# One down tile of each small expert slot in native fp32, an eighth load buffer, and a token table reduced earlier

## The chip, the cores and the metric

The kernel runs on one core of a Trainium2 chip. The metric is the device time of one execution in microseconds (us). The engines are PE (TensorE, matrix products, with its weight loads PEld), DVE (VectorE), ACT (ScalarE), POOL (GpSimd) and SP (SyncE, which only issues transfers here).

## The reference

One decoder block: 512 tokens and 16 meta tokens of width 1024 go through a hybrid mixer (FoX attention and RWKV-7 side by side), then through a mixture of 32 experts of which each token takes four, with LayerNorm after each. The change lies in the mixture:

```python
def moe_ffn(h, w_router, b_router, w_gu, b_gu, w_down, b_down):
    logits = (h @ w_router + b_router).astype(jnp.float32)
    top_vals, top_idx = lax.top_k(logits, TOP_K)
    gates = jax.nn.softmax(top_vals, axis=-1)
    ...
    def expert_block(args):
        xblk, e = args
        gu = xblk @ w_gu[e] + b_gu[e]
        gate, up = gu[:, :D_EXPERT], gu[:, D_EXPERT:]
        gate = jnp.minimum(gate, SWIGLU_LIMIT)
        up = jnp.clip(up, -SWIGLU_LIMIT, SWIGLU_LIMIT)
        act = (up + 1.0) * (gate * jax.nn.sigmoid(gate * SWIGLU_ALPHA))
        return act @ w_down[e] + b_down[e]
```

Everything is float32. Each expert has 1024 x 2048 gate and up weights (8 MB) and 1024 x 1024 down weights (4 MB), so 384 MB of weights pass through the core.

## The kernel before, in words

The mixer takes the first 480 us or so. After it the router ranks the experts, tokens are entered in a table by expert, and the 32 experts are worked through as 32 *slots*, sorted by their number of tokens. `KINDS = "BBS" + "SB" * 14 + "B"` (L43) names them: a big slot (B) holds up to 112 tokens, a small one (S, 15 of them: slots 2, 3, 5, 7, ... 29) up to 64. From slot 3 on a small and a big slot take turns; such a pair is the unit in which the trace repeats.

*Tiles.* A slot has eight gate/up tiles, called ko0 to ko7 (`gtile`, L1427), and four down tiles, c0 to c3 (`dtile`, L1437). Each is 128x2048 float32, 1 MB, and is loaded by SP into a `raw` buffer. Seven such buffers are used in turn: `RAW = 5` in one pool and `RAW2 = 2` in another.

*Split.* float32 products are made from two fp32r parts. `split_w` (L1013) writes the high part `wh` with a copy on ACT (recorded at L130) and the low part `wl = raw - wh` with a subtraction on DVE (L1019); there are five buffers for each. A `raw` buffer is free once the subtraction has read it. `spl` holds the last two split instructions.

*Matmuls.* All go through the helper `mm` (L100). In a big slot the activations also have a high and a low part, and a product takes three passes. In a small slot the high and low parts of 64 tokens stand side by side as 128 stationary columns, so that two passes (`wh`, `wl`) do; rows 0 to 63 of the result hold the product with the high part, rows 64 to 127 that with the low part, and `put` adds them.

*A slot's turn* (the loop from L1722): the gate/up matmuls (`gu_stage`); the splits of down tiles c0 and c1 of the slot before (`PD = 2`); the activation, `swiglu` for a big slot (ACT `sgm`, DVE `act` at L1482 and L1483), `halves` for a small one; the transposes of the next slot's tokens (`flip_pair` gives `xs` for a small slot, `flip` gives `xTh` and `xTl` for a big one); then the down matmuls of the slot before, with the splits of c2 and c3 (`down_stage`); the splits of the next slot's ko0 and ko1 (`PG = 2`); and `put`, which scales the result by the gates and adds it to the output by an indirect DMA on POOL (L1569). For a small slot `put` is two instructions on ACT (`yl`) and two on DVE (`yo`, L1566). Last comes the second half of the activation: `flip` of `act` (PE transposes, then `aTh` on ACT, `aTl` on DVE at L1387) for a big slot, `swiglu_pair` for a small one, which ends in `at` (128 x 8 x 64, float32) and `a2`, its high and low part.

*What sets the order.* A scheduler orders each engine's instructions within the data dependences; `order(i, j)` puts i behind j, and `held` puts the activation and `put` behind the last split (`hold`), so that the splits run ahead.

*The table.* Tokens are scattered in rounds into four tables, which POOL copies into `tab4`. In slot 0's turn `listed` (L1361) reduces them on DVE over the four tables: a minimum gives the token numbers, a maximum the gates:

```python
V.tensor_reduce(lst[:, 0], tab4[:, :, :, 0].rearrange("p k c -> p c k"), AX.X, OP.min)
V.tensor_reduce(lst[:, 1], tab4[:, :, :, 1].bitcast(F32).rearrange("p k c -> p c k"), AX.X, OP.max)
```

`take` (L1276) makes `xTh`, `xTl` of slots 0 and 1. `xz` (L1310) is a zeroed tile that ACT's queue writes to the padding rows of two DRAM tensors, 512 KB each. The one-hot tile `ohs` (`onehot`, L1372) serves the last slots.

Of the kernel before, what the change touches and what calls it, by code (L numbers as in the profile page):

```python
# [9 lines left out]
F32 = mybir.dt.float32  # L10
F32R = mybir.dt.float32r
# [12 lines left out]
D = 1024  # L24
# [41 lines left out]
FAFTER = (0, 1, 3)  # L66
FOXG = (2, 4, 8, 8)
RAW = 5
RAW2 = 2
MLO = 3  # L70
MLL = 2
MHI = 3
# [2 lines left out]
PRE = 8  # L75
PD = 2
PG = 2

C_MU, C_W0, C_A0, C_KK, C_KA, C_RK, C_BF, C_G0, C_B0, C_G1, C_B1, C_N = 0, 14, 18, 22, 26, 30, 34, 35, 43, 51, 59, 67

# [13 lines left out]
def hybrid_block(ctx, tc, x, meta, win, wf, wout, cvec, lw, g2, lnp, gnp, wr, br,  # L94
# [4 lines left out]
    def mm(o, l, r, start, stop):  # L99
        return T.matmul(o, l, r, start=start, stop=stop, skip_group_check=True)  # L100
# [1169 lines left out]
    xp = pool(ctx, "xT", 2, "right")  # L1270
    mhr = pool(ctx, "mhr", MHR, "right")

    def xt_tile():
        return [xp.tile([128, KO, 128], F32R, tag=n, name=n) for n in ("xTh", "xTl")]

    def take(ps):  # L1276
        xT = xt_tile()
        for f0 in (0, 4):
            pv = ps[f0 // 4].rearrange("p (a b) -> p a b", b=128)
            a = actv(xT[0][:, f0:f0 + 4], pv, AF.Copy)  # L1280
            v = V.tensor_tensor(xT[1][:, f0:f0 + 4], pv, f32(xT[0][:, f0:f0 + 4]), OP.subtract)
        return xT, a, v

    xT, xci, xvi = take(ps0)
    xT1 = take(ps1)[0]
    rp = bank()
    for j in range(4):
        mm(rp[:, 0:NE], oneb, selb[:, j, :], j == 0, j == 3)
# [69 lines left out]
        V.tensor_copy(eidt, ps[0:1, 2 * NE:3 * NE])  # L1358
        V.tensor_copy(capr, ps[:, NE:2 * NE])

    def listed():  # L1361
        lst = mp2.tile([NE, 2, C], F32, name="lst")
        V.tensor_reduce(lst[:, 0], tab4[:, :, :, 0].rearrange("p k c -> p c k"), AX.X, OP.min)
        V.tensor_reduce(lst[:, 1], tab4[:, :, :, 1].bitcast(F32).rearrange("p k c -> p c k"), AX.X, OP.max)
        ps = small_ps()
        for j in range(2):
            mm(ps[0:C, NE * j:NE * j + NE], lst[:, j], perm, True, True)
        V.tensor_copy(idxs[0:C], ps[0:C, 0:NE])
        V.tensor_copy(gates[0:C], ps[0:C, NE:2 * NE])
        V.tensor_copy(gates[H:2 * H, NE - NSM:], ps[0:H, 2 * NE - NSM:2 * NE])  # L1370
# [16 lines left out]
            tail[3] = V.tensor_tensor(lo[:, f0:f0 + 4], pv, f32(h), OP.subtract)  # L1387
        return hi, lo

    xgt = xp.tile([128, D], F32, name="xg", bufs=1)  # L1390
    G.memset(xgt, 0.0)

    def fetch(idx, n):
# [43 lines left out]
    def dtile(sl, c):  # L1437
        raw = raw_tile()
        nc.sync.dma_start(raw, w_down[expert(sl), c].rearrange("o p n -> p (o n)"))
        after = None  # L1440
        if sl == NE - 2 and c == 3:
            after = (None, tail[0])
        if sl == NE - 1 and c:
            after = (tail[2] if c > 1 else None, tail[3])
        dw[sl, c] = split_w(raw, after)

    def gu_stage(sl, xT):
        small = KINDS[sl] == "S"
# [25 lines left out]
    hold = [None, None]  # L1474

    def swiglu(ps):
        act = wk.tile([128, D], F32, tag="act", name="act")[0:C]
        for n in range(2):
            s = slice(512 * n, 512 * n + 512)
            sg = wk.tile([128, 512], F32, tag="sgm", name="sgm", bufs=2)[0:C]  # L1480
            held(actv(sg, ps[n], AF.Silu, scale=SALPHA), 0)
            held(V.tensor_scalar(act[:, s], ps[2 + n], 1.0 - LIM, 1.0 + LIM, op0=OP.max, op1=OP.min), 1)  # L1482
            tail[0] = V.scalar_tensor_tensor(act[:, s], sg, SALPHA * LIM * SIGLIM, act[:, s], op0=OP.min, op1=OP.mult)  # L1483
        return act
# [7 lines left out]
    def swiglu_pair(gt):  # L1492
        pt = []
        for j in range(2):
            ps = psT.tile([128, 512], F32, tag="tr", name="tr")
            for f in range(KO):
                mm(ps[:, H * f:H * f + H], gt[:, D * j + 128 * f:D * j + 128 * f + 128], fold, True, True)
            pt.append(ps)
        sg = wk.tile([128, 512], F32, tag="sgm", name="sgp", bufs=2)
        actv(sg, pt[0], AF.Silu, scale=SALPHA)  # L1500
        at = wk.tile([128, D], F32, tag="act", name="at")[:, 0:512]
        V.tensor_scalar(at, pt[1], 1.0 - LIM, 1.0 + LIM, op0=OP.max, op1=OP.min)
        V.scalar_tensor_tensor(at, sg, SALPHA * LIM * SIGLIM, at, op0=OP.min, op1=OP.mult)
        a2 = wk.tile([128, KO, 2, H], F32R, tag="aTh", name="a2")
        av = at.rearrange("p (k c) -> p k c", c=H)
        actv(a2[:, :, 0, :], av, AF.Copy)
        V.tensor_tensor(a2[:, :, 1, :], av, f32(a2[:, :, 0, :]), OP.subtract)
        return a2

    def down_stage(sl, aT):  # L1510
        small = KINDS[sl] == "S"
        pl, rows_ = PLACE[sl], 128 if small else C
        ps = [psD.tile([128, 512], F32, tag="dn", name="dn")[0:rows_] for _ in range(2)]
        for c in range(4):
            if (sl, c) not in dw:
                dtile(sl, c)
            w = dw.pop((sl, c))
            for k in range(2):
                for a, b in ((0, 0), (1, 0)) if small else PASS:
                    for n in range(2):  # L1520
                        st_ = aT[:, 2 * c + k].rearrange("p a c -> p (a c)") if small else aT[b][:, 2 * c + k, :]
                        i = mm(ps[n], st_, w[a][:, D * k + 512 * n:D * k + 512 * n + 512],
                               c == k == a == b == 0, c == 3 and k == 1 and a == 1)
                        if sl == NE - 2 and c == 3 and k == a == b == n == 0:
                            order(i, tail[1])
        return ps, gates[0:rows_, pl:pl + 1], idxs[0:H if small else C, pl:pl + 1]
# [195 lines left out]
    for sl in range(NE):  # L1722
        nxt = KINDS[sl + 1] if sl + 1 < NE else None
        if sl and nxt:
            n, pl = H if nxt == "S" else C, PLACE[sl + 1]
            xg = fetch(idxs[0:n, pl:pl + 1], n)
        if sl == NE - 2:
            oh = onehot(FIXED[2], G)
        small, final = KINDS[sl] == "S", sl == NE - 1
        gu = gu_stage(sl, xT)  # L1730
        if sl == 0:
            ranked()
            listed()
        if pend is not None:
            for c in range(PD):
                dtile(pend[0], c)
            hold[:] = spl
        act = (halves if small else swiglu)(gu)
        if sl == PRE:
            prepare()  # L1740
        if sl == 0:
            xT = xT1
        elif nxt:
            xT = flip_pair(xg) if nxt == "S" else flip(xg, [t[:, :, 0:C] for t in xt_tile()])
        if final:
            aT = flip(act, [t[:, :, 0:C] for t in xt_tile()])
        if pend is not None:
            dn = down_stage(*pend)
            if nxt:
                for k in range(PG):  # L1750
                    gtile(sl + 1, k)
                hold[:] = spl
            else:
                hold[:] = [None, None]
            put(*dn, KINDS[pend[0]] == "S")
        pend = (sl, aT if final else swiglu_pair(act) if small else flip(act))
        if sl == TBL:
            tables()
# [83 lines left out]
```

## Time and profile before

| | |
|---|---|
| median of three runs | 1661.18 us (1655.45 to 1666.61) |
| profiled execution | 1652.43 us, of which its span is 1650.7 us |
| mean granted TensorE clock | 0.961 |
| busy share of the span | PE 92%, DVE 82%, ACT 63%, POOL 20% |
| bytes moved | 470 MB in all, mean 285 GB/s |

The profiled execution lies 8.75 us under the median of the runs and just below the fastest of them. The table shows averages; the mixer and the slots have different limits, so that the slots have to be read by themselves.

### The profile page before, as it was taken

What the parts mean: (1) busy time and instruction counts of PE and PEld (TensorE: products, weight loads), DVE (VectorE), ACT (ScalarE), POOL (GpSimd) and SP (SyncE); (2) the same over time, 40 slices, a digit from 0 to 9 for tenths busy, and PEclk for the clock granted to TensorE, in tenths of its full rate; (3) what the DMA queues carried; (4) which work ended last, traced back from release to release, by engine and by line L of the source; (5) the groups of instructions that cost most, each with busy time, mean ns of one, the idle gap of its engine ahead of it and who ended that gap; (6) DMA issues with size and microseconds to landing.
All of it is one profiled execution on the core that took longest, in us unless ns stands there. A gap on an engine that the chain in (4) does not pass through costs nothing.

```text
span 1650.7 us, 22742 instructions
## 1 busy us (share of the span) xinstructions
PE 1525.8 (92%) x8375; PEld 1199.1 (73%) x8375; DVE 1352.7 (82%) x1470; ACT 1036.9 (63%) x1059; POOL 327.6 (20%) x236
## 2 busy tenths in 40 slices
PE   4999999999997999999999999999999999999992
PEld 3799997786785777677676776767767677676761
DVE  8377584477887989988989889898898988989884
ACT  4444232234335778787877777777777777777762
POOL 5011201024443415111111111111211112111002
PEclk9799995799998999999999999999999999999996
DMA  4222313002667999999999999999999999999963
GB/s 180 75 77 77 79 52 84 1 20 88 243 210 269 324 382 418 403 397 381 383 386 393 375 369 391 388 396 370 375 393 382 396 369 375 386 385 389 372 227 128
DMA packets 89236, 469.90 MB, mean 285 GB/s; under 512 B 21676, under 2 KB 22716, under 8 KB 39938
## 3 DMA queue, kind: packets, MB, share of 16 engines
q1 hardware_dynamic: 76608, 444.51, 69.3%
q0 software_dynamic: 7136, 19.42, 5.2%
q10 hardware_dynamic: 5378, 4.50, 1.0%
q8 instruction: 67, 1.10, 0.3%
q14 instruction: 47, 0.39, 0.1%
HBM read 446.78 MB, written 24.53 MB: 286 GB/s over the span
## 4 chain that ended last, share of the span: by engine, by line
PE 32%; DVE 19%; issue 10%; ACT 3%; DMA 3%; POOL 0%; DVEq 0%; POOLq 0%; ACTq 0%
PE gu L100 18%; DVE wl L1019 15%; PE dn L100 10%; PE tr L100 3%; ACT wh L130 2%; DMA raw<-in_w_gu_dram 2%; DVE yo L1566 1%; DVE act L1483 1%; DMA raw<-in_w_down_dram 1%; DVE xTl L1387 1%; DVE aTl L1387 1%; ACT sgm L130 0%; PE tr L1403 0%; PE pc L100 0%; ACT raw L130 0%
## 5 line engine op out<-in xcount | busy, mean ns | idle before, releaser
L1019 DVE TENSOR_TENSOR wl<-raw,wh 128x2048 fp32r<-128x2048 f32 x384 | 859.8, 2282 | 93.7 <-ACT wh L130 92.5
L130 ACT ACTIVATE wh<-raw 128x2048 fp32r<-128x2048 f32 x384 | 709.7, 1914 | 46.1 <-PE gu L100 13.5
L1569 POOL DMA_INDIRECT yd<-yo,idxs x31 | 81.8, 2640 | 573.0 <-DVE yo L1566 404.3
L100 PE MATMUL gu<-wl,xs 128*128 128x512 f32 x480 | 142.5, 418 | 33.8 <-DVE wl L1019 28.7
L100 PE MATMUL gu<-wl,xTh 128*112 128x512 f32 x544 | 149.6, 394 | 9.0 <-DVE wl L1019 9.0
L1395 POOL DMA_INDIRECT xg<-h1d,idxs x30 | 84.7, 2823 | 339.5 <-PE tr L1403 297.9
L100 PE MATMUL gu<-wh,xTh 128*112 128x512 f32 x544 | 150.4, 395 | 0.4 <-ACT wh L130 0.4
L100 PE MATMUL gu<-wh,xTl 128*112 128x512 f32 x544 | 148.8, 393 | 0.0
L100 PEld LDWEIGHTS gu<-wl,xs 128*128 128x128 f32 x480 | 81.7, 188 | 87.8 <-DVE wl L1019 76.0
L100 PE MATMUL gu<-wh,xs 128*128 128x512 f32 x480 | 133.2, 399 | 6.8 <-ACT wh L130 6.8
L100 PE MATMUL acc<-hTh,wh 128*128 128x264 f32 x416 | 121.2, 293 | 8.1 <-DVE zk L361 2.9
L100 PEld LDWEIGHTS gu<-wl,xTh 128*112 128x112 f32 x544 | 94.9, 175 | 39.7 <-DVE wl L1019 10.4
L100 PE MATMUL acc<-hTl,wh 128*128 128x264 f32 x416 | 120.6, 291 | 1.0 <-DVE hTl L312 1.0
L100 PE MATMUL acc<-hTh,wl 128*128 128x264 f32 x416 | 120.7, 291 | 0.0
L100 PEld LDWEIGHTS gu<-wh,xTh 128*112 128x112 f32 x544 | 95.1, 175 | 31.0 <-ACT wh L130 0.9
L100 PEld LDWEIGHTS gu<-wh,xTl 128*112 128x112 f32 x544 | 95.3, 175 | 30.6
L100 PEld LDWEIGHTS gu<-wh,xs 128*128 128x128 f32 x480 | 88.3, 188 | 31.5 <-ACT wh L130 12.4
L100 PEld LDWEIGHTS acc<-hTh,wh 128*128 128x128 f32 x416 | 79.3, 191 | 10.9 <-ACT hTh L130 2.9
L100 PE MATMUL dn<-wl,aTh 128*112 128x512 f32 x256 | 83.7, 408 | 1.1
L100 PE MATMUL dn<-wh,aTh 128*112 128x512 f32 x256 | 81.5, 399 | 0.0
L100 PEld LDWEIGHTS acc<-hTl,wh 128*128 128x128 f32 x416 | 79.5, 191 | 2.3 <-DVE hTl L312 1.8
L130 ACT ACTIVATE wh<-rawA 128x512 fp32r<-128x512 f32 x52 | 32.2, 627 | 76.5 <-PE acc L100 62.5
(519 smaller groups left out, 2523.8 us busy)
## 6 DMA issues: line engine op xcount, KB each, us to landing
raw<-in_w_gu_dram SPq DMA_DIRECT2D x256, 1024.0 KB, 9.0
raw<-in_w_down_dram SPq DMA_DIRECT2D x128, 1024.0 KB, 8.3
rawA<-in_win_dram SPq DMA_DIRECT2D x26, 512.0 KB, 3.3
wor<-in_wout_dram SPq DMA_DIRECT2D x8, 512.0 KB, 5.9
xt<-in_x_dram SPq DMA_DIRECT2D x4, 512.0 KB, 6.1
hd<-h SPq DMA_DIRECT2D x4, 512.0 KB, 3.0
hres<-hd SPq DMA_DIRECT2D x4, 512.0 KB
h1d<-h SPq DMA_DIRECT2D x4, 512.0 KB, 4.7
```

The source lines that it names most:

```text
L100: return T.matmul(o, l, r, start=start, stop=stop, skip_group_check=True)
L130: last[0] = S.activation(*a, **k)
L1019: ins.append(V.tensor_tensor(lo, raw, f32(hi), OP.subtract))
L1387: tail[3] = V.tensor_tensor(lo[:, f0:f0 + 4], pv, f32(h), OP.subtract)
L1395: G.indirect_dma_start(out=xg, out_offset=None, in_=h1d[0:NT], in_offset=bass.IndirectOffsetOnAxis(ap=idx, axis=0), bounds_check=NT - 1, o ...
L1483: tail[0] = V.scalar_tensor_tensor(act[:, s], sg, SALPHA * LIM * SIGLIM, act[:, s], op0=OP.min, op1=OP.mult)
L1566: held(V.scalar_tensor_tensor(yo[:, hs], ps[n][0:H], ga[0:H], yl, op0=OP.mult, op1=OP.add), 1)
L1569: G.indirect_dma_start(out=yd, out_offset=bass.IndirectOffsetOnAxis(ap=si, axis=0), in_=yo, in_offset=None, compute_op=OP.add)
```

## The change

Down tile c2 of each small slot (`NAT = (2,)`) isn't split any more. `down_stage` takes its `raw` buffer as it is, with `at` as 64 float32 stationary columns: four matmuls of 128x512 (two halves of the rows by two halves of the columns) into rows 0 to 63 of the result, where the split tile took eight. `at` has to live longer for that and moves from the buffer `act` to the buffer `ohs`.

`RAW2` goes from 2 to 3: an eighth `raw` buffer. Its room is found by sharing: `xTl` gets one buffer instead of two, with the low part of slot 1's tokens in `yo`; the gathered tokens `xg` move to the buffer `act`, and `act` to the buffer `gt`.

`listed` gets an argument: the first of its two reductions is put behind `last_w`, the last split of slot 0's gate/up tiles.

```diff
-RAW2 = 2
+RAW2 = 3
+NAT = (2,)
...
-    def listed():
+    def listed(after):
         lst = mp2.tile([NE, 2, C], F32, name="lst")
-        V.tensor_reduce(lst[:, 0], tab4[:, :, :, 0].rearrange("p k c -> p c k"), AX.X, OP.min)
+        i = V.tensor_reduce(lst[:, 0], tab4[:, :, :, 0].rearrange("p k c -> p c k"), AX.X, OP.min)
+        order(i, after)
         V.tensor_reduce(lst[:, 1], tab4[:, :, :, 1].bitcast(F32).rearrange("p k c -> p c k"), AX.X, OP.max)
...
-        dw[sl, c] = split_w(raw, after)
+        dw[sl, c] = raw if KINDS[sl] == "S" and c in NAT else split_w(raw, after)
...
-        act = wk.tile([128, D], F32, tag="act", name="act")[0:C]
+        act = fwk.tile([128, 2 * D], F32, tag="gt", name="act", bufs=1)[0:C, 0:D]
...
-        at = wk.tile([128, D], F32, tag="act", name="at")[:, 0:512]
+        at = wk.tile([128, 512], F32, tag="ohs", name="at")
...
-            for k in range(2):
+            for k in range(2) if small and c in NAT else ():
+                f = H * (2 * c + k)
+                for n in range(2):
+                    mm(ps[n][0:H], aT[1][:, f:f + H], w[:, D * k + 512 * n:D * k + 512 * n + 512], False, False)
+            for k in () if small and c in NAT else range(2):
...
+            last_w = spl[1]
             ranked()
-            listed()
+            listed(last_w)
```

What it moves. First DVE in the turn of a big slot whose predecessor is small, from the activation `act` to the gate/up splits of the next small slot. Before:

```order
L1482 TENSOR_SCALAR act<-gu 112x512 x2
L1019 TENSOR_TENSOR wl<-raw,wh 128x2048
L1483 SCALAR_TENSOR_TENSOR act<-sgm,act 112x512 x2
L1019 TENSOR_TENSOR wl<-raw,wh 128x2048 x3
L1566 SCALAR_TENSOR_TENSOR yo<-dn,gates,yl 64x512 x2
L1387 TENSOR_TENSOR aTl<-tr,aTh 128x4x112 x2
L1019 TENSOR_TENSOR wl<-raw,wh 128x2048 x2
L1387 TENSOR_TENSOR xTl<-tr,xTh 128x4x112 x2
L1019 TENSOR_TENSOR wl<-raw,wh 128x2048 x8
```

After:

```order
L1485 TENSOR_SCALAR act<-gu 112x512 x2
L1486 SCALAR_TENSOR_TENSOR act<-sgm,act 112x512 x2
L1020 TENSOR_TENSOR wl<-raw,wh 128x2048 x3
L1573 SCALAR_TENSOR_TENSOR yo<-dn,gates,yl 64x512 x2
L1390 TENSOR_TENSOR aTl<-tr,aTh 128x4x112 x2
L1020 TENSOR_TENSOR wl<-raw,wh 128x2048 x2
L1390 TENSOR_TENSOR xTl<-tr,xTh 128x4x112 x2
L1020 TENSOR_TENSOR wl<-raw,wh 128x2048 x8
```

The subtraction of c2, which stood between the two halves of `act`, is gone; the three behind it (c3, ko0, ko1) and all the rest stand as they did.

Second PE in the same place, from the bias matmuls of the next small slot (`gu<-bh`) over the end of the small slot's down matmuls (`dn`) to its first gate/up tile (`gu<-wh,xs`); `tr<-ident,act` are the transposes of `act`. Before:

```order
L100 MATMUL gu<-bh,selb_4372 128x512 x2
L100 MATMUL dn<-wl,a_9505 128x512 x2
L100 MATMUL dn<-wh,a_9505 128x512 x2
L100 MATMUL dn<-wl,a_9505 128x512 x2
L100 MATMUL dn<-wh,a_9505 128x512 x2
L1383 MATMUL tr<-ident,act 128x112 x8
L100 MATMUL gu<-wh,xs 128x512 x4
L100 MATMUL dn<-wl,a_9505 128x512 x2
L100 MATMUL dn<-wh,a_9505 128x512 x2
L100 MATMUL dn<-wl,a_9505 128x512 x2
L100 MATMUL gu<-wl,xs 128x512 x4
```

After:

```order
L101 MATMUL dn<-wl,a_9967 128x512 x2
L101 MATMUL dn<-raw,at 64x512 x4
L101 MATMUL gu<-bh,selb_4372 128x512 x2
L1386 MATMUL tr<-ident,act 128x112 x8
L101 MATMUL dn<-wh,a_9967 128x512 x2
L101 MATMUL dn<-wl,a_9967 128x512 x2
L101 MATMUL dn<-wh,a_9967 128x512 x2
L101 MATMUL dn<-wl,a_9967 128x512 x2
L101 MATMUL gu<-wh,xs 128x512 x4
L101 MATMUL gu<-wl,xs 128x512 x4
```

The four native matmuls stand between c1 and c3, and the first gate/up pass `gu<-wh,xs` now stands behind the last down pair instead of ahead of the last three.

Third DVE in slot 0's turn, where the two reductions stand among slot 0's splits. Before:

```order
L1281 TENSOR_TENSOR xTl<-acc,xTh 128x512 x2
L1345 TENSOR_SCALAR kc<-kc 32x1
L1019 TENSOR_TENSOR wl<-raw,wh 128x2048 x2
L1363 TENSOR_REDUCE lst<-tab_5288 32x112
L1364 TENSOR_REDUCE lst<-tab_5288 32x112
L1019 TENSOR_TENSOR wl<-raw,wh 128x2048 x8
L1482 TENSOR_SCALAR act<-gu 112x512 x2
```

After:

```order
L1283 TENSOR_TENSOR x1l<-acc,xTh 128x512 x2
L1347 TENSOR_SCALAR kc<-kc 32x1
L1020 TENSOR_TENSOR wl<-raw,wh 128x2048 x2
L1367 TENSOR_REDUCE lst<-tab_5288 32x112
L1020 TENSOR_TENSOR wl<-raw,wh 128x2048 x4
L1365 TENSOR_REDUCE lst<-tab_5288 32x112
L1020 TENSOR_TENSOR wl<-raw,wh 128x2048 x4
L1485 TENSOR_SCALAR act<-gu 112x512 x2
```

The minimum (now L1365) moved behind slot 0's four last splits; the maximum (now L1367) stayed where both stood.

Smaller moves: the zeroing of `xz` on POOL now waits for the end of slot 1's gate/up matmuls, and its two writes are issued by ACT between the two `sgm` of slot 1 instead of ahead of slot 0; the one-hot tile of the last slot is made on POOL in slot 30's turn; and SP may issue one load of slot 0 earlier.

## Rows read from the trace of the kernel before

**Rows 1.** The page: busy time, share and instructions of each engine.

```profile
PE 1525.8 (92%) x8375; PEld 1199.1 (73%) x8375; DVE 1352.7 (82%) x1470; ACT 1036.9 (63%) x1059; POOL 327.6 (20%) x236
```

**Rows 2.** Windows: us, busy (instructions) PE, PEld, DVE, ACT, POOL; clock, DMA share, GB/s.

```profile
526.00:540.00 14.00, 13.63 (x64) 10.23 (x63) 13.80 (x22) 5.70 (x5) 3.62 (x1) 1.00 1.01 426
...
931.00:1000.00 69.00, 65.78 (x305) 49.41 (x305) 61.62 (x38) 52.74 (x41) 10.24 (x4) 1.00 1.00 382
```

**Rows 3.** Chain of waits, 900 to 1000 us: start, us, engine, operand, line.

```profile
939.56 4.31 DVE wl L1019 x2
...
978.68 21.39 PE gu L100 x93
```

**Rows 4.** PE's timeline, one pair, from the small slot's down matmuls on.

```profile
931.52 0.62 PE L100 MATMUL dn<-wh,a 128*128 128x512 f32 x2
...
938.42 0.93 PE L1383 MATMUL tr<-ident,act 112*128 112x112 f32 x8
939.12 1.17 PE L100 MATMUL gu<-wh,xs 128*128 128x512 f32 x4
...
941.06 0.62 PE L100 MATMUL dn<-wl,a 128*128 128x512 f32 x2
...
961.78 0.62 PE L100 MATMUL dn<-wh,aTh 128*112 128x512 f32 x2
```

**Rows 5.** DVE's timeline in that pair; brackets: idle time before, and what ended it.

```profile
931.49 1.29 DVE L1482 TENSOR_SCALAR act<-gu 112x512 f32<-112x512 f32 x2 [1.05 <-PE gu L100]
933.95 2.29 DVE L1019 TENSOR_TENSOR wl<-raw,wh 128x2048 fp32r<-128x2048 f32 x1 [1.17 <-ACT wh L130]
...
937.36 6.69 DVE L1019 TENSOR_TENSOR wl<-raw,wh 128x2048 fp32r<-128x2048 f32 x3
943.97 1.39 DVE L1566 SCALAR_TENSOR_TENSOR yo<-dn,gates,yl 64x512 f32<-64x512 f32 x2
...
946.35 4.47 DVE L1019 TENSOR_TENSOR wl<-raw,wh 128x2048 fp32r<-128x2048 f32 x2
...
951.82 15.66 DVE L1019 TENSOR_TENSOR wl<-raw,wh 128x2048 fp32r<-128x2048 f32 x7
```

**Rows 6.** ACT's timeline, that pair and the two last of the same kind.

```profile
931.02 1.08 ACT L130 ACTIVATE sgm<-gu 112x512 f32<-112x512 f32 x2 [5.32 <-PE gu L100]
...
941.54 1.26 ACT L130 ACTIVATE yl<-dn,gates 64x512 f32<-64x512 f32 x2 [2.22 <-issue]
...
943.83 3.72 ACT L130 ACTIVATE wh<-raw 128x2048 fp32r<-128x2048 f32 x2
...
1552.32 1.09 ACT L130 ACTIVATE sgm<-gu 112x512 f32<-112x512 f32 x2 [5.29 <-PE gu L100]
...
1584.70 1.08 ACT L130 ACTIVATE sgm<-gu 112x512 f32<-112x512 f32 x2 [4.04 <-PE gu L100]
```

**Rows 7.** PE's and PEld's timeline: unsplit float32 matmuls of the mixer.

```profile
325.91 0.30 PEld L100 LDWEIGHTS m<-g2t,zg 128*128 128x128 f32 x2
...
336.11 1.08 PE L100 MATMUL o<-vmbd,pm 128*128 128x512 f32 x2
337.03 0.97 PE L100 MATMUL s<-kmbd,qT 128*128 128x32 f32 x8
...
402.60 1.08 PE L100 MATMUL o<-vmbd,pm 128*128 128x512 f32 x2
403.61 0.67 PE L100 MATMUL m<-UV,Q 64*64 64x64 f32 x8
```

**Rows 8.** DVE's timeline at the token table, slot 0.

```profile
514.07 0.91 DVE L1363 TENSOR_REDUCE lst<-tab 32x112 f32<-32x448 int32 x1 [8.38 <-DMA tab<-tab]
```

**Rows 9.** Waits, 528 to 654 us: us in total, times, longest.

```profile
ACT wh L130 <- DMA raw<-in_w_gu_dram: 5.9, 5, 1.6
...
PE dn L100 <- DVE wl L1019: 1.6, 1, 1.6
...
PE gu L100 <- DVE wl L1019: 0.9, 2, 0.5
```

More of the change, by code (lines that the diff above doesn't have):

```diff
@@ L1271, in hybrid_block, with xt_tile, take @@
     mhr = pool(ctx, "mhr", MHR, "right")
[L1273 to L1277, printed above, removed]
+    def xt_tile(lo=None):
+        hi = xp.tile([128, KO, 128], F32R, tag="xTh", name="xTh")
+        return [hi, xp.tile([128, KO, 128], F32R, tag="xTl", name="xTl", bufs=1) if lo is None else lo]
+    def take(ps, lo=None):
+        xT = xt_tile(lo)
         for f0 in (0, 4):
@@ L1284, in hybrid_block @@
     xT, xci, xvi = take(ps0)
-    xT1 = take(ps1)[0]
+    xT1 = take(ps1, mw.tile([128, KO, 128], F32R, tag="yo", name="x1l"))[0]
     rp = bank()
@@ L1388, in flip @@
         return hi, lo
-    xgt = xp.tile([128, D], F32, name="xg", bufs=1)
+    xgt = wk.tile([128, D], F32, tag="act", name="xg")
     G.memset(xgt, 0.0)
@@ L1507, in swiglu_pair @@
         V.tensor_tensor(a2[:, :, 1, :], av, f32(a2[:, :, 0, :]), OP.subtract)
-        return a2
+        return a2, at
     def down_stage(sl, aT):
@@ L1517, in down_stage @@
             w = dw.pop((sl, c))
-            for k in range(2):
+            for k in range(2) if small and c in NAT else ():
[3 more added lines that the diff above has]
+            for k in () if small and c in NAT else range(2):
                 for a, b in ((0, 0), (1, 0)) if small else PASS:
                     for n in range(2):
-                        st_ = aT[:, 2 * c + k].rearrange("p a c -> p (a c)") if small else aT[b][:, 2 * c + k, :]
+                        st_ = aT[0][:, 2 * c + k].rearrange("p a c -> p (a c)") if small else aT[b][:, 2 * c + k, :]
                         i = mm(ps[n], st_, w[a][:, D * k + 512 * n:D * k + 512 * n + 512],
```

## Prediction, written before the changed kernel had run

> **What bounds the kernel now.** The page comes first [rows 1]: PE is busy for 92% of the span, DVE for 82%. That is an average over a mixer and 32 slots, so the slots are read by themselves. A big and a small slot together, a pair, repeat: the `sgm` that opens the small slot's down phase starts at 931.02 us and, nine pairs later, at 1552.32 [rows 6], so a pair takes 621.30 / 9 = 69.03 us. In one pair's window PE is busy for 65.78 of 69 us at full clock, DVE for 61.62, ACT for 52.74 [rows 2]. PE and DVE are both nearly full; which of them sets the pace has to be seen by phase.
>
> The chain of waits answers that [rows 3]. In the second part of the pair it runs through 93 gate/up matmuls in a row (21.39 us): there PE is the bound. In the first part it runs through DVE's `wl`. That first part begins when the big slot's gate/up matmuls end and the small slot's down matmuls start (931.52, called t0) and ends when the big slot's down matmuls start (961.78) [rows 4]; 30.26 us. PE's timeline gives what a pair of matmuls costs: from t0 to the last down pair at 941.06 PE issues 15 down pairs, two bias pairs, one gate/up group (two pairs) and eight transposes. The transposes take 939.12 - 938.42 = 0.70 us, which leaves 8.84 us for 19 pairs, 0.465 us each [rows 4]. All 16 down pairs, two bias pairs, 32 gate/up pairs and two sets of transposes make 50 x 0.465 + 1.4 = 24.7 us, so about 5.6 us of the first part is PE waiting.
>
> DVE has no such room there [rows 5]. From t0: the two halves of `act` around `wl` of c2 (931.49 to 937.36, with 1.17 us of waiting for `wh` in it), `wl` of c3, ko0 and ko1 (6.69 us), `yo` at 943.97, `aTl`, `wl` of ko2 and ko3 from 946.35, `xTl`, and from 951.82 `wl` one after the other; ko7's ends four subtractions of 2.24 us later, at 960.8, where PE's last gate/up group starts. So the chain to shorten is DVE's, and c2 is on it.
>
> **The change part by part.** I work in the profiled execution's time (1652.43 us). The median of the runs is 8.75 us higher; I add the differences to the median.
>
> *Native c2, 13 pairs (the down matmuls of small slots 3, 5, ... 27).* Removed in the first part: one `wl` of 2.29 us and the wait of 1.17 us ahead of it on DVE [rows 5], one `wh` of 7.33 / 4 = 1.83 us on ACT [rows 6], and eight split matmuls, four pairs, 1.86 us, on PE. DVE then finishes ko1 at 943.97 - 2.2 - 1.17 = about 940.6. Added on PE: four native matmuls. The trace has unsplit float32 matmuls of the same 128x512 shape in the mixer; the record counts two for each matmul, and from its start to that of the next group it takes 0.92 us in one place and 1.01 in another [rows 7]. Four cost N = 3.68 to 4.04 us.
>
> What is late next is PE's own down phase. `yo` reads `yl`, and `yl` on ACT reads the end of the small slot's down product. Before, the last down pair starts at t0 + 9.54 [rows 4]. After, there stand ahead of it eight pairs of c0 and c1, three of c3, two of bias, the eight transposes and the four native ones: 13 x 0.465 + 0.70 + N = 6.74 + N; the gate/up group now stands behind it. With N = 3.68 that is t0 + 10.42, 0.88 us later than before. So DVE stands idle for over 2 us ahead of `yo`, and everything behind `yo` and `yl` moves with PE. Some of it is slack: `yl` (941.54), two `aTh` and the two `wh` from 943.83 finish ko2's high part at 943.83 + 1.86 = 945.69, and DVE takes up ko2 at 946.35 [rows 5, 6]: 0.66 us to spare. Behind that point DVE's queue is unchanged. Per pair the change is therefore
>
> N + 6.74 - 9.54 - 0.66 = N - 3.46 us: +0.22 at the lower price, +0.58 at the higher.
>
> I take the lower, since 3.68 stands on a matmul with the same neighbours on both sides, and a stationary operand of 64 columns should not load slower than one of 128: 13 x 0.22 = **+2.9 us** (up to +7.5). In the second part of the pair nothing is touched, and the chain there is PE's.
>
> *The two small slots outside the pairs.* Slot 2's down matmuls run while PE is nearly always busy (13.63 of 14 us in one window [rows 2]), so the matmuls themselves count: N - 1.86 = **+1.8 us**. Slot 29's are followed by a big slot and not a small one. PE's work in that phase after the change, 12 down pairs, N, two bias pairs and transposes, and 96 gate/up matmuls at 21.39 / 93 = 0.23 us [rows 3], is 5.58 + 3.68 + 0.93 + 0.70 + 22.08 = 32.97 us, against 1584.70 - 1552.32 = 32.38 us that the phase lasts now [rows 6]: **+0.6 us**.
>
> *The token table.* Before, the minimum waits 8.38 us for the table copies on DVE's queue, then takes 0.91 us [rows 8], and slot 0's remaining eight subtractions stand behind it. By the order the maximum stays where it was, ahead of these subtractions, and it reads the same copies. So the 8.38 us wait is still there, with another instruction at its end; only the minimum's 0.9 us leaves the way of slot 0's splits: **-0.9 us**. If the wait moved as well, it would be up to -9.3.
>
> *The eighth buffer, xz.* What a further load ahead can give is bounded by PE's waits for splits behind late loads. Between 528 and 654 us ACT waits for `raw` loads 5.9 us for gate/up tiles [rows 9], but PE waits for DVE's `wl` only 1.6 and 0.9 us: at most -2.5. In the pairs no load is waited for. Against it stand the two 512 KB writes of `xz`, which move from ahead of slot 0 into this stretch, where loads run at 426 GB/s [rows 2]: 1.05 MB, 2.5 us of transfer, and ACT now issues them between slot 1's two `sgm`, so that the second `sgm`, `act` and the splits behind them wait for POOL's zeroing and for a queue. PE has slot 0's down tiles, split by then, to work on. I take 0, with ends of -2.5 and +3. The buffers that are now shared hold nothing that is still read when the next user comes in the steady pairs: `act` goes into `gt` after the small slot's last read of it, `at` into `ohs`, which is otherwise used only at the end. The c2 buffer is freed by PE instead of DVE, some 2 us later, with one buffer more in turn.
>
> *Sum:* 2.9 + 1.8 + 0.6 - 0.9 + 0 = **+4.4 us**: 1656.8 in the profiled execution's time, 1661.2 + 4.4 = **1665.6 us** as a median. Its own range: with N at 4.04, +7.5 + 2.2 + 1.0 - 0.9 + 3 = +12.8; with N at 4 x 0.86 (each 0.06 under the lower row), 13 x -0.02, +1.6, +0.4, -0.9 and -2.5, about -1.7; and the three runs scatter by some 5 us about their median. So 1655 to 1679.
>
> **The rivals.**
>
> *A. DVE's relief counts in full (faster).* The first part is DVE's, so taking 2.2 us from its queue shortens each pair by 2.2: 13 x -2.2 = -28.6, with the other terms (+1.5) -27.1, 1634 us; with the wait of 1.17 us gone as well, -42, 1619. For it: the chain [rows 3] and PE's 5.6 us of waiting. Against it: `yo` can't come before the last down pair. It needs N under 3.46 - 2.2 = 1.26 us, a third of what the rows show [rows 7]; or a matmul with 64 stationary columns that is far cheaper than one with 128, which this trace does not show. 0.17.
>
> *B. The native matmuls cost more, and PE becomes the bound (slower).* In the mixer, the next weight load may lie under the matmul before; between fp32r and float32 it may not. If each native matmul shows its load of 0.30 us [rows 7], four take 4 x 1.22 = 4.9 us: 13 x 1.44 = +18.7, slot 2 +3.0, slot 29 +1.8, -0.9: +22.6, 1684 us. It decides by itself, over 1%, from about 4.5 us for four (13 x 1.04 + 2.6 + 1.4 - 0.9 = 16.6), 1.13 us each. Against it: the mixer's matmuls alternate operands, too, and stay at 0.92 to 1.01. 0.14.
>
> *C. The table part does what its words say.* If the maximum's place by the scheduler's list costs no wait, 9.3 us of slot 0's stall leaves: +4.4 - 8.4 = -4.0, 1657 us. Against it: both reductions read the four copies. 0.05.
>
> *D. Transfers set the pace in the pairs.* The DMA share is 1.00 there, at 382 GB/s [rows 2]; then neither engine's change matters, and +1.5 us is left: 1663. Against it: 426 GB/s were moved elsewhere, and at that rate the pair's 382 x 69 = 26.4 MB take 62 us, not 69. 0.05.
> The Trainium skill ("Perfetto Trace Analysis", "Engine Utilization") gives 358 GB/s as a core's share of the memory and about 435 GB/s as the most that the 16 DMA engines of a core alone move; by the first the pairs would be transfer-bound and rival D hold, by the second they are at 88% of the limit. The trace has 426 GB/s in one stretch, so the second agrees and the first does not bind here.
>
> **How the numbers follow.** Forecast 0.59 (1665.6), A 0.17 (1634), B 0.14 (1684), C 0.05, D 0.05. A change of 1%, 16.6 us, is about what a measurement of this kernel tells from none. Faster by over 1% is A: 0.17; slower by over 1% is B, most of it: 0.13 and 0.02 from the forecast's upper edge, 0.15; within 1% the rest, 0.68. The range leaves out the far half of A and of B: from 1640 to 1683; the forecast's own range inside it is 1655 to 1679.
>
> **What would show it.** In the changed profile: native matmuls at 0.92 us spacing (8 records for four); DVE idle for 2 to 3 us ahead of `yo`, released by ACT's `yl`; the last down pair about 0.9 us later after t0; a pair of 69.2 to 69.6 us; the 8.4 us wait of DVE for the table copies, now at the maximum; 15 fewer `wl` and `wh`. It is wrong if the pair falls to 67 us with no wait ahead of `yo` (A), if a native matmul takes 1.13 us or more (B), if PE no longer idles at the table (C), or if the pair's length does not move while `yo` does (D).

## The result, and the profile after

The changed kernel takes 1670.89 us (median of 22 runs, 1661.79 to 1679.50), the kernel before 1656.69 us in the runs beside it (22 runs, 1648.67 to 1669.43): a ratio of 1.0079 (95% interval 1.0058 to 1.0099), 13.1 us more on 1656.7, between 9.6 and 16.4 (the two medians differ by 14.2). The forecast was +4.4, and all ratios below are to the kernel before.

The profiled execution has a span of 1670.6 us, 19.9 more than before, and a reader has to take that apart first. About half of it lies ahead of the first instruction that the change moves. The row below is the same instruction near the mixer's end in both kernels, one of DVE's first on the router's logits: 444.32 us before, 454.33 after.

DVE's timeline of the kernel before:

```profile
444.32 4.35 DVE L1193 SCALAR_TENSOR_TENSOR lg<-lg,lnry,wcs 128x32 f32<-128x32 f32 x1
```

The changed kernel's:

```profile
454.33 4.48 DVE L1194 SCALAR_TENSOR_TENSOR lg<-lg,lnry,wcs 128x32 f32<-128x32 f32 x1
```

Up to there every engine's instructions stand in the same order in both. The difference is TensorE's granted clock: between 340 and 360 us its mean was 1.00 before and 0.71 after (eighth column, ahead of DMA share and GB/s), so that the same work took longer. The 0.71 is a mix: 0.50, the lower of the clock's two levels (1.2 GHz), from 335 to 350 us, and 0.91 in the ten microseconds behind; PE was busy nearly without a break in both kernels. Windows of the kernel before, then of the changed one:

```profile
320.00:340.00 20.00, 19.63 (x148) 16.06 (x147) 10.13 (x26) 6.65 (x23) 2.27 (x3) 0.87 0.00 1
340.00:360.00 20.00, 20.00 (x187) 16.11 (x186) 17.17 (x46) 8.11 (x31) 10.64 (x12) 1.00 0.08 28
```

```profile
320.00:340.00 20.00, 20.00 (x135) 17.01 (x135) 9.54 (x25) 5.40 (x16) 2.27 (x3) 0.70 0.00 1
340.00:360.00 20.00, 19.63 (x133) 15.72 (x133) 10.76 (x32) 5.54 (x23) 8.57 (x9) 0.71 0.02 8
```

In the twelve traces of this study the instruction just ahead of that one (`lg<-wcs`) begins between 443.6 and 455.2 us. The eight kernels made from the changed one spread over 444.2 to 455.2 (mean 449.9), the four made from the kernel before over 443.6 to 446.1 (mean 444.4). Whether a few microseconds of that belong to the change, by where its buffers lie, these single executions can't tell; it stays open. So traces are compared from that point on, and whole kernels by the ratio of many runs.

From there on, 9.9 us are left, and the stages of the two traces place them (starts of `sgm`, the activation of a big slot; the first stage is counted from `lg<-wcs`, at 444.04 and 454.05 us):

| stage | before, us | after, us | difference |
|---|---|---|---|
| `lg` to slot 0's `sgm` | 86.76 | 86.03 | -0.7 |
| to slot 1's | 26.47 | 25.72 | -0.8 |
| to slot 4's (slots 2 and 3) | 96.93 | 98.04 | +1.1 |
| to slot 30's (13 pairs) | 898.12 | 908.37 | +10.3 |
| to slot 31's | 32.38 | 33.06 | +0.7 |
| to slot 31's `yh`, its scaled result | 30.29 | 29.63 | -0.7 |

The pairs are the result; the other stages differ as much between executions of the same instructions, as the part on the prediction shows. The page and the window of one pair show that PE works more and DVE less [rows 1, 2]:

```profile
PE 1561.9 (93%) x8375; PEld 1202.1 (72%) x8375; DVE 1321.7 (79%) x1455; ACT 1010.2 (60%) x1044; POOL 278.7 (17%) x236
```

```profile
944.00:1014.00 70.00, 67.77 (x307) 49.28 (x306) 59.73 (x38) 50.81 (x40) 8.00 (x4) 1.00 0.98 381
```

ACT's `sgm` and `yl` answer to [rows 6]: nine pairs in 1572.21 - 944.35 = 627.86 us, 69.76 each against 69.03.

```profile
944.35 1.08 ACT L131 ACTIVATE sgm<-gu 112x512 f32<-112x512 f32 x2 [5.32 <-PE gu L101]
...
955.81 1.26 ACT L131 ACTIVATE yl<-dn,gates 64x512 f32<-64x512 f32 x2 [4.97 <-PE dn L101]
...
1572.21 1.08 ACT L131 ACTIVATE sgm<-gu 112x512 f32<-112x512 f32 x2 [5.35 <-PE gu L101]
```

PE's timeline of the same pair answers to [rows 4]. t0 is now 944.85. The eight records from 949.04 are the four native matmuls: 952.62 - 949.04 = 3.58 us, 0.90 each.

```profile
944.85 0.62 PE L101 MATMUL dn<-wh,a 128*128 128x512 f32 x2
...
949.04 3.65 PE L101 MATMUL dn<-raw,at 128*64 128x512 f32 x8
952.62 0.73 PE L101 MATMUL gu<-bh,selb 128*128 128x512 f32 x2
953.19 0.93 PE L1386 MATMUL tr<-ident,act 112*128 112x112 f32 x8
...
955.37 0.62 PE L101 MATMUL dn<-wl,a 128*128 128x512 f32 x2
...
975.49 0.62 PE L101 MATMUL dn<-wh,aTh 128*112 128x512 f32 x2
```

The second part of the pair changed, too, although the diff touches nothing in it. The transposes of `gt` stand in other groups between the big slot's down matmuls. From the first of those (961.78 [rows 4], 975.49 after) to the next big slot's first gate/up matmul it takes 16.73 us before and 17.02 after. PE before, then after:

```profile
966.95 1.00 PE L100 MATMUL tr<-fold,gt 128*128 128x64 f32 x8
...
978.51 1.08 PE L100 MATMUL gu<-wh,xTh 128*112 128x512 f32 x4
```

```profile
980.62 1.45 PE L101 MATMUL tr<-fold,gt 128*128 128x64 f32 x12
...
992.51 1.08 PE L101 MATMUL gu<-wh,xTh 128*112 128x512 f32 x4
```

DVE's timeline answers to [rows 5]. It comes to `yo` early and stands idle for 2.56 us until ACT's `yl`, then for 1.05 us more until `wh` of ko2.

```profile
944.81 1.29 DVE L1485 TENSOR_SCALAR act<-gu 112x512 f32<-112x512 f32 x2 [0.66 <-PE gu L101]
946.02 1.28 DVE L1486 SCALAR_TENSOR_TENSOR act<-sgm,act 112x512 f32<-112x512 f32 x2
947.27 6.70 DVE L1020 TENSOR_TENSOR wl<-raw,wh 128x2048 fp32r<-128x2048 f32 x3
956.52 1.40 DVE L1573 SCALAR_TENSOR_TENSOR yo<-dn,gates,yl 64x512 f32<-64x512 f32 x2 [2.56 <-ACT yl L131]
957.85 1.14 DVE L1390 TENSOR_TENSOR aTl<-tr,aTh 128x448 fp32r<-128x448 f32 x2
960.04 4.49 DVE L1020 TENSOR_TENSOR wl<-raw,wh 128x2048 fp32r<-128x2048 f32 x2 [1.05 <-ACT wh L131]
```

At the table the wait that stood at the minimum [rows 8] stands at the maximum:

```profile
523.98 0.91 DVE L1367 TENSOR_REDUCE lst<-tab 32x112 f32<-32x448 f32 x1 [8.72 <-DMA tab<-tab]
```

### The profile page after: what moved, and what is told of

Its sections match the earlier page's. It is cut to its first block, busy times and chain, and to the rows that moved or that the text cites. A ratio compares the mean times of both kernels' runs of the same rounds, so it can differ in the third digit from the quotient of the medians.

```text
span 1670.6 us, 22697 instructions
## 1 busy us (share of the span) xinstructions
PE 1561.9 (93%) x8375; PEld 1202.1 (72%) x8375; DVE 1321.7 (79%) x1455; ACT 1010.2 (60%) x1044; POOL 278.7 (17%) x236
## 5 line engine op out<-in xcount | busy, mean ns | idle before, releaser
L1020 DVE TENSOR_TENSOR wl<-raw,wh 128x2048 fp32r<-128x2048 f32 x369 | 824.5, 2286 | 74.0 <-ACT wh L131 72.8
L131 ACT ACTIVATE wh<-raw 128x2048 fp32r<-128x2048 f32 x369 | 679.2, 1913 | 34.5 <-PE gu L101 13.4
L1398 POOL DMA_INDIRECT xg<-h1d,idxs x30 | 76.5, 2549 | 382.1 <-PE tr L1406 318.0
L101 PE MATMUL gu<-wh,xTl 128*112 128x512 f32 x512 | 139.0, 393 | 0.0
L1576 POOL DMA_INDIRECT yd<-yo,idxs x31 | 47.8, 1540 | 545.4 <-DVE yo L1573 415.3
L101 PEld LDWEIGHTS gu<-wh,xs 128*128 128x128 f32 x480 | 88.9, 188 | 30.2 <-ACT wh L131 10.3
L101 PEld LDWEIGHTS gu<-wh,xTl 128*112 128x112 f32 x512 | 89.6, 175 | 28.8
L101 PEld LDWEIGHTS acc<-hTh,wl 128*128 128x128 f32 x416 | 80.2, 193 | 0.6
```

The source lines that it names most:

```text
L131: last[0] = S.activation(*a, **k)
L1020: ins.append(V.tensor_tensor(lo, raw, f32(hi), OP.subtract))
L1398: G.indirect_dma_start(out=xg, out_offset=None, in_=h1d[0:NT], in_offset=bass.IndirectOffsetOnAxis(ap=idx, axis=0), bounds_check=NT - 1, o ...
L1576: G.indirect_dma_start(out=yd, out_offset=bass.IndirectOffsetOnAxis(ap=si, axis=0), in_=yo, in_offset=None, compute_op=OP.add)
```

## The experiments

The theory: the native matmuls make the end of the small down product late, `yl`, `aTh` and the next `wh` on ACT follow it, and DVE's relief turns into waiting. Rivals: the loss comes from the shared buffers or the table; DVE's chain rules whatever PE does.

**Without the native tile.**

```diff
-NAT = (2,)
+NAT = ()
```

> The changed kernel with every down tile split again; the eighth buffer, the shared buffers and the moved minimum stay. Theory (the native matmuls make the small down product late, and yl, yo and the next splits with it): the pair goes back from about 69.8 us to 69.0, slots 2 and 29 give back 1.8 and 0.6, so the time comes back to that of the kernel before, within 3 us (ratio 0.998 to 1.002). Rival (the shared buffers or the moved table work cost the time): pairs stay at 69.6 us or more and the ratio stays near 1.008.

Measured: 1648.17 us, ratio 0.9954 (0.9923 to 0.9986): faster than the kernel before by 7.6 us. Neither theory nor rival had expected that; the pair is not 69.0 but 68.1 us. The native tile is to blame for the loss, and for more of it than the result shows: something else in the change gains. DVE's order there, both halves of `act` and then four subtractions without a wait:

```profile
936.35 1.28 DVE L1486 SCALAR_TENSOR_TENSOR act<-sgm,act 112x512 f32<-112x512 f32 x2
937.60 8.90 DVE L1020 TENSOR_TENSOR wl<-raw,wh 128x2048 fp32r<-128x2048 f32 x4
```

**The native tile alone.** Seven load buffers again, the minimum not ordered; the shared buffers stay.

```diff
-RAW2 = 3
+RAW2 = 2
...
-        order(i, after)
```

> The changed kernel with seven load buffers again and the minimum not ordered: the native tile and the shared buffers alone. Theory: pairs of 69.7 to 69.9 us and a ratio of 1.007 to 1.009, as with the whole change. Rival (the native tile is about neutral, the loss comes with the eighth buffer or the table): pairs near 69.1 us, ratio within 0.002 of 1.

Measured: ratio 1.0049 (1.0021 to 1.0077), pairs of 69.4 to 69.5 us. That lies between theory and rival: with the shared buffers alone beside it, the native tile costs 0.4 us a pair, and with the eighth buffer the pair is another 0.3 us longer.

**One native matmul of four, and each twice.** These two change N alone.

```diff
-                for n in range(2):
+                for n in range(1 - k):
```

> The changed kernel with one native matmul instead of four in each small slot; three quarters of tile c2's product are left out. Theory (the end of PE's down phase releases yl and yo): the last down pair comes 2.75 us earlier, DVE's wait ahead of yo goes from 2.56 us to about none, and the pair falls by about 2.75 us to 67.0, which makes some 40 us in all. Rival (DVE's chain sets the phase whatever PE does): the pair stays within 0.5 us of 69.7.

```diff
+                    for _ in range(2):
```

> The changed kernel with each native matmul issued twice, so that c2's product counts double. Theory: DVE's wait ahead of yo grows by the 3.6 us that four more matmuls take, the pair goes to about 73.3 us, and the time rises by 13 x 3.6 + 2 x 3.6 = 54 us. Rival (PE has room in this phase, its 5.6 us of waiting): the pair grows by less than 1 us, under 15 us in all.

Measured: 1632.91 us (two runs), 38 us less than the change, and 1719.17 us (two runs), 48 more (54 expected). The pairs took 67.2 and 73.2 us. DVE's wait at `yo`, none with one matmul, is 5.99 us with eight; with one, DVE still waits 1.06 us for ACT's `wh` of ko2, which stands behind `yl`. DVE's timeline with one matmul, then with eight:

```profile
937.75 6.69 DVE L1020 TENSOR_TENSOR wl<-raw,wh 128x2048 fp32r<-128x2048 f32 x3
944.43 1.40 DVE L1573 SCALAR_TENSOR_TENSOR yo<-dn,gates,yl 64x512 f32<-64x512 f32 x2
...
947.95 4.49 DVE L1020 TENSOR_TENSOR wl<-raw,wh 128x2048 fp32r<-128x2048 f32 x2 [1.06 <-ACT wh L131]
```

```profile
961.06 6.70 DVE L1020 TENSOR_TENSOR wl<-raw,wh 128x2048 fp32r<-128x2048 f32 x3
973.75 1.40 DVE L1574 SCALAR_TENSOR_TENSOR yo<-dn,gates,yl 64x512 f32<-64x512 f32 x2 [5.99 <-ACT yl L131]
```

That DVE's chain rules whatever PE does is refuted: in these kernels the first part of the pair moves with the last down pair, -2.56 us for -2.56 and +3.44 for +3.45.

**The transposes of `act` behind the last down matmul.**

```diff
+                if late is not None:
+                    order(tp, late)
...
```

(`late` is the small slot's last down matmul, `tp` each transpose.)

> The changed kernel with PE's eight transposes of act behind the small slot's last down matmul instead of ahead of tile c3. Theory (the end of PE's down phase releases yl and yo): the last down pair comes 0.8 us earlier, the pair falls by 0.7 to 0.8 us to 69.1, 10 us in all, ratio 1.001 to 1.003. Rival (aTh and aTl, now later, hold the next splits up as much): pairs within 0.2 us of 69.8.

Measured: ratio 0.9996 (0.9972 to 1.0020), pair 69.0 us, 0.79 us less than in the change. The theory holds in the other direction, too: with nothing computed differently, an earlier last down pair gives its time back.

**Both reductions behind slot 0's splits.**

```diff
-        V.tensor_reduce(lst[:, 1], ...
+        i = V.tensor_reduce(lst[:, 1], ...
+        order(i, after)
```

> The changed kernel with the maximum, too, behind slot 0's last split. Theory (the maximum that stayed in its place waits for the table copies in the minimum's stead): DVE's wait of 8.7 us and PE's idle time of 8.1 us in slot 0 go, and with them the low clock behind it; 8 to 11 us less than the change, a ratio of 1.001 to 1.003 to the kernel before; pairs unchanged at 69.8 us. Rival (slot 0 and 1 are held up by loads, or the copies only move their wait to slot 1's splits): under 3 us.

Measured: ratio 1.0065 (1.0040 to 1.0091), pairs of 69.8 us. The expected 8 to 11 us did not come; against the change's 1.0079 nothing is certain. In the profiled execution the wait itself is gone (526.00 follows six subtractions without a break), and from slot 0's first gate/up matmul to its `sgm` it takes 25.4 us instead of the change's 34.7. But that first matmul comes 57.4 us after `lg` and not 51.3: between 500 and 510 us, where PE gathers slot 0's tokens (`gu<-oh,h1h`), the granted clock was 0.50, the lower level (1.2 GHz), and 1.00 in the change's profile. So 3.3 us are left of the gain here. What the other executions gained isn't shown; the run after next has a profile in which the wait only moved.

```profile
512.79 13.28 DVE L1020 TENSOR_TENSOR wl<-raw,wh 128x2048 fp32r<-128x2048 f32 x6
526.00 0.99 DVE L1365 TENSOR_REDUCE lst<-tab 32x112 f32<-32x448 int32 x1
```

**The order of c2's subtraction alone, in the kernel before.** What made the run without native tiles faster? Its DVE does both halves of `act` first and then four subtractions; the kernel before has c2's subtraction between the halves, with the 1.17 us wait ahead of it [rows 5]. The scheduler chose that other order with eight buffers. The kernel before with that one order added:

```diff
+        if KINDS[sl] == "S" and c == 2:
+            after = (None, tail[0])
```

> The kernel before (seven buffers, all tiles split) with one line more: the low part of each small slot's c2 is put behind the second half of act on DVE. The run without native tiles had that order, a pair of 68.1 us and no 1.17 us wait ahead of c2's subtraction. Theory (that order, which the scheduler chose with eight buffers, is what made it faster, and not the buffer): the first part of the pair falls by 1.2 us, the pair to 67.8 to 68.0, 14 to 16 us in all, ratio 0.990 to 0.992. Rival (the eighth buffer's earlier loads did it): the pair stays at 69.0, ratio 1.000.

Measured: ratio 0.9954 (0.9926 to 0.9981), pair 68.5 us. Rival refuted: seven buffers with the order gain as well. But the pair fell by 0.6 us only, and DVE's timeline says why: `yo` comes 1.2 us earlier, then 0.53 us are lost again at ko2, whose `wh` stands behind `yl` and `aTh` on ACT.

```profile
934.51 8.90 DVE L1019 TENSOR_TENSOR wl<-raw,wh 128x2048 fp32r<-128x2048 f32 x4
943.32 1.39 DVE L1568 SCALAR_TENSOR_TENSOR yo<-dn,gates,yl 64x512 f32<-64x512 f32 x2
944.64 1.14 DVE L1387 TENSOR_TENSOR aTl<-tr,aTh 128x448 fp32r<-128x448 f32 x2
946.31 4.49 DVE L1019 TENSOR_TENSOR wl<-raw,wh 128x2048 fp32r<-128x2048 f32 x2 [0.53 <-ACT wh L130]
```

**That order and both reductions, in the kernel before.**

> The kernel before with that order of c2's subtraction and with both reductions behind slot 0's last split: no native tile, no eighth buffer. Theory: both gains add, 14 to 16 us in the pairs and 8 to 11 at the table, 22 to 27 us less than before, ratio 0.984 to 0.987. Rival (the table's gain is lost to loads): 0.990 to 0.992.

Measured: ratio 0.9943 (0.9921 to 0.9966), 1649.66 us, no better than the order alone (1648.12). Here the rows show what became of the table's gain: slot 0's `sgm` comes 8.3 us earlier after `lg` than before, but slot 1's then follows it 37.1 us later instead of 26.5. POOL's last scatter into the token table lasts 14.37 us, and DVE then waits 11.01 us for the copies behind it. POOL's and DVE's timelines of this kernel:

```profile
500.59 14.37 POOL L1232 DMA_INDIRECT tab<-ent,pos  x1 [0.30 <-issue]
```

```profile
500.84 13.28 DVE L1019 TENSOR_TENSOR wl<-raw,wh 128x2048 fp32r<-128x2048 f32 x6
525.13 0.91 DVE L1363 TENSOR_REDUCE lst<-tab 32x112 f32<-32x448 int32 x1 [11.01 <-DMA tab<-tab]
```

The kernel before has two subtractions at that place and a scatter of 5.55 us:

```profile
500.98 5.55 POOL L1232 DMA_INDIRECT tab<-ent,pos  x1 [0.30 <-issue]
```

```profile
501.22 4.47 DVE L1019 TENSOR_TENSOR wl<-raw,wh 128x2048 fp32r<-128x2048 f32 x2
```

In both, the scatter ends 0.84 us after the last subtraction of the run that began beside it (506.53 after 505.69, 514.96 after 514.12). Four more subtractions ahead of the reductions made the scatter longer by as much, and the wait moved instead of going. In the profiled execution of the run with both reductions in the changed kernel, the scatter was over at 512.23, before DVE's run began at 512.79, and no wait was left:

```profile
510.13 2.10 POOL L1233 DMA_INDIRECT tab<-ent,pos  x1 [0.30 <-issue]
```

The other traces agree. In nine of the twelve the row of subtractions began beside this scatter, 0.24 to 0.26 us after it, and the scatter outlasted it (5.55 or 5.56 us with two, 14.37 with six); in three the scatter was over before the row began (2.09 or 2.10 us). So it matters whether the scatter is done when the row starts.

**Two orders in the kernel before.** The second puts PE's first gate/up group of the next small slot behind the last down pair, as the changed kernel's scheduler had done:

```diff
...
+                    if small and sl > 4 and ko == a == 0:
+                        order(i, dlast[0])
...
```

(besides the order of c2's subtraction, the rest of the diff left out; `dlast[0]` is the last down matmul, `i` the gate/up matmul.)

> The kernel before with two orders more: c2's subtraction behind the second half of act (as in the run with that order alone), and PE's first gate/up group of the next small slot behind the last down pair. So far the first part of the pair has been the last down pair's time plus 20.1 us, unless DVE came later. Theory: the last down pair comes at 8.65 instead of 9.56 us, yl no longer holds the next split, DVE's chain alone is left, and the first part takes 29.1 us as in the run without native tiles, the second 38.8 as in the kernel before: a pair of 67.8 to 67.9 us, 15 us less than before, ratio 0.990 to 0.992. Rival (the second order gives nothing, since the gate/up group it moves is then late itself): 68.4 us as with the first order alone, ratio 0.995.

Measured: 1646.10 us, ratio 0.9914 (0.9885 to 0.9942), pair 67.8 us, as expected. It beats both kernels, without a native tile and without an eighth buffer.

**Half a native tile, late transposes.** Two native matmuls, the other half of c2 split, and the transposes of `act` behind the last down matmul:

```diff
-        dw[sl, c] = raw if KINDS[sl] == "S" and c in NAT else split_w(raw, after)
+        if KINDS[sl] == "S" and c in NAT:
+            hi, lo = split_w(raw, after, slice(D, 2 * D))
+            dw[sl, c] = hi, lo, raw
...
```

> The changed kernel with half of tile c2 native (two matmuls; the other half split) and the transposes of act behind the small slot's last down matmul. Theory (last down pair plus 20.1 us): 15 pairs of matmuls and two native ones put the last down pair at 9.0 us, the first part takes 29.1 and the second 39.1 us, a pair of 68.2 us; ratio 0.995 to 0.997, no better than the kernel without native tiles. Rival (DVE's relief of 1.1 us shows as well): 67.6 us or less.

Measured: ratio 0.9934 (0.9898 to 0.9969), pair 68.2 us: the pair as expected, the ratio a little better, its interval reaching to 0.9969. It can't be told from the kernel without native tiles (0.9954). DVE's relief doesn't show, so the rival is refuted.

**All runs together.** Read from PE's timeline in one pair of each (starts between 927 and 959 us): the last down pair and the end of the first part, counted from t0; their difference; the second part.

| kernel | last down pair | first part | difference | second part |
|---|---|---|---|---|
| before | 9.54 | 30.26 | 20.72 | 38.79 |
| changed | 10.52 | 30.64 | 20.12 | 39.01 |
| without native tile | 8.62 | 29.04 | 20.42 | 39.10 |
| native tile alone | 10.53 | 30.65 | 20.12 | 38.75 |
| one native matmul | 7.96 | 28.08 | 20.12 | 39.01 |
| eight native matmuls | 13.97 | 34.08 | 20.11 | 39.02 |
| both reductions | 10.53 | 30.65 | 20.12 | 39.03 |
| late transposes | 9.75 | 29.87 | 20.12 | 39.02 |
| c2's order | 9.56 | 29.68 | 20.12 | 38.78 |
| c2's order, reductions | 9.56 | 29.66 | 20.10 | 38.81 |
| two orders | 8.63 | 29.06 | 20.43 | 38.80 |
| half native, late transposes | 8.95 | 29.08 | 20.13 | 39.11 |

In nine kernels the first part is the last down pair plus 20.1 us: the path over `yl`, `aTh` and ko2's `wh` on ACT binds. In three, all with c2 split whole, it is longer and DVE's own chain binds: by 0.60 us in the kernel before, where the prediction read 0.66 us of slack, and by 0.3 in the two whose last down pair comes at 8.6. The second part is 38.75 to 38.81 with seven buffers and 39.01 to 39.11 with eight. That holds with and without a native tile, and with seven buffers whether or not the table's reductions are moved.

## Why the prediction was right or wrong

*The range held, in part by luck.* 1670.89 us lies within 1655 to 1679, but the change was sized at a third of what it is. The range's upper end was made mostly of a native price (4.04 us) that was not met and a cost of `xz` (+3) that no run shows, and the pairs' term passed the end that it was given: 10.3 us against at most 7.5, a pair of 69.76 us against 69.2 to 69.6. The absolute time came closer (5.3 us off) than the difference (8.7 us off), since the three runs that it was set on had a median 4.5 us above that of the 22.

*What binds, and what would be late next: right.* DVE's relief became a wait of 2.56 us ahead of `yo`, released by `yl` (2 to 3 us predicted); the last down pair came 0.98 us later after t0 (0.9 predicted); the slack, read as 0.66 us, is the difference between 20.72 and 20.12, 0.60.

*N: right, its surroundings a little too cheap.* 3.58 us for four native matmuls, 0.90 each, where 0.92 and 1.01 were the rows [rows 7]. Their weight loads don't show, so rival B's price did not come. The changes between kinds of matmul around them do cost something: the pair ahead of the native ones takes 949.04 - 948.50 = 0.54 us and the bias pair behind 0.57, where 0.465 was reckoned, 0.18 together. The first part grew by 0.38 us in the pair that was read, 0.44 on the mean of nine, instead of 0.22.

*"In the second part of the pair nothing is touched": wrong, and this is the step, with the price of those changes, that made the pairs' term too small.* The diff touches nothing there, but with eight buffers PE's transposes and matmuls stand in another order, and the part takes 0.22 us more (39.01 against 38.79), 0.29 on the mean of nine. The rows place it in the stretch with the changed order, 16.73 us before and 17.02 after; the gate/up matmuls behind it take 22.1 and 22.0 us. No run has that order with seven buffers, so that the order is the cause is argued. With 0.38 + 0.22 = 0.60 us in the pair that was read and 0.73 on the mean of nine, the term "13 x 0.22 = +2.9 us" came out at 9.5 to 10.3.

*The eighth buffer at 0: wrong in kind.* I bounded it by waits for loads, -2.5 to +3. The whole of what the change does without its native tile is worth -7.6 us, and the profile has it in the pairs: 888.9 us from slot 4's `sgm` to slot 30's, against 898.1 before. DVE does c2's subtraction behind both halves of `act`, the wait of 1.17 us is gone, and the gate/up group stands behind the last down pair. The same two orders by hand, with seven buffers, give as much and more. In the change as it stands the native tile takes that gain up, since it removes the same wait and sets a later one: against the changed kernel without it, it costs 30.64 - 29.04 = 1.6 us a pair, some 20 us in all (1.0079 against 0.9954).

*The table: right about the wait, open in size.* The 8.4 us wait stayed, at the maximum (8.72). The way to slot 0's activation became 0.7 us shorter (0.9 predicted), but one profile doesn't size it: five more kernels with the changed one's table order take 80.4 to 84.5 us over that stage, where it took 86.0, and four with the old kernel's 86.6 to 86.9. "Up to -9.3 if the wait moved as well" was too simple: moved whole, it gave nothing that the runs can tell.

*Slots 2 and 29: near in these two profiles, not shown.* The stage of slots 2 and 3 grew by 1.1 us (1.8 predicted), but by 1.2 to 4.0 in the three other kernels with four native matmuls. The stage of slot 29's down phase grew by 0.7 (0.6 predicted), but without the native tile by 1.1, so that native matmuls in place of split ones are not what made it longer. The sum of +4.4 missed 13.1 mostly by the pairs' term, 7 us of it. The rest, 13.1 against the 9.9 us that the stages show, lies within the interval, and may be the mixer's.

*The rivals.* A (DVE's relief counts) fell with the wait ahead of `yo`. Even where N is about 1 us, in the run with one native matmul, the first part is the last down pair plus 20.12 us: DVE finds `yl` ready but waits for `wh` behind it. B fell with 0.90 us a matmul. C fell with the wait at the maximum. D fell since the pair follows PE's down phase one for one: at 381 GB/s in the change, and at 396 with one native matmul.

## What to carry to other kernels

Work taken from the engine that binds a phase is worth no more than the slack of the next path to the same instruction; here both were legible beforehand, 0.66 us and N - 3.46. One formula (last down pair plus 20.1 us) then carried over nine kernels. A change between kinds of matmul has a price of its own. Where a scheduler sets the order, a change of a pool's size is a change of order: compare the order of the whole steady pair, also where the diff says nothing, and look for a wait that a different order alone removes, since that came cheaper here than any new arithmetic. And split such a change in two before judging it: one half cost 20 us and hid the other half's 7.6.

## What the runs showed of the hardware

An indirect scatter on POOL that started 0.25 us ahead of a row of DVE subtractions was not done until 0.84 us after the last of them: 5.55 us with two and 14.37 us with six. The one ahead of it, which met a single subtraction, took 2.92 us in the kernel before; scatters of that round that met none took 0.95 to 1.08 us. The Trainium skill ("SBUF — State Buffer", "Who interferes with whom") says that a DVE instruction with two inputs in SBUF contends with a GpSimd instruction that reads SBUF. The trace agrees that the two collide, and the scatter was held off over six instructions in a row; that shared access to SBUF is the reason isn't shown here.

Four float32 matmuls with 64 stationary columns and 512 moving ones took 3.58 us at a granted clock of 1.00, 0.90 each, against 0.465 for two fp32r ones; going over to them and back cost 0.18 us together.

The mixer, with the same instructions in the same order, took from 444.2 to 455.2 us in the eight kernels made from the changed one, with stretches of lower granted clock in different places: 11 us between single profiles, about what the change itself costs. They can be compared only stage by stage.
